# A gate summed on VectorE, spreads by high and low parts, and longer runs of column-tiled products in a two-layer trunk

## The chip, the cores and the metric

The kernel runs on one core of a Trainium2 chip. The core has TensorE (matrix products; PE in the profile, its weight loads PEld), VectorE (DVE), ScalarE (ACT), GpSimd (POOL) and SyncE (SP, which here only issues DMA). The metric is the device time of one execution in microseconds: lower is better. Times of several runs are given as a median with the lowest and highest.

## The reference, cut to what matters

Two layers run over x, 256 tokens of width 1024, all in fp32. In each layer a conditioning vector gives a shift, a scale and a gate, each of 1024 values:

```python
cond = jax.nn.silu(c)
for i in range(DEPTH):                      # DEPTH = 2
    shift, scale, gate = jnp.split(cond @ ada_w[i] + ada_b[i], 3, axis=-1)
    h = rms_norm(x, norm_g[i]) * (1 + scale[:, None, :]) + shift[:, None, :]
    y = nsa_mixer(h, ...) if i % 2 == 0 else moba_mixer(h, ...)
    x = x + gate[:, None, :] * y
```

The first layer's mixer projects h to queries, three kinds of keys and values, branch gates and z. It attends to compressed blocks, to selected blocks and to a window (with 256 tokens the selected blocks and the window both come to causal attention), adds the three with the branch gates, multiplies by silu(z) and projects out. The second layer's mixer has one kind of keys and values and, at this length, is plain causal attention with 16 query heads over 4 key heads of 64, again with silu(z) and an output projection. `cond @ ada_w[i]` reads 12 MB of weights in each layer.

## The kernel before, in words

**Layout.** 128 partitions carry tokens (two tiles `m` of 128) or, where h is transposed (`HT`), channels. Weights come as pieces of 512 KB into a ring of six buffers `raw` (in the opening into twelve buffers `early`). A product of precision fp32 is made of three products of the type fp32r: a value is split into a high part (`hi`, a cast on ScalarE) and a low part (`lo`, a subtraction on VectorE), and high by high, high by low and low by high are added (`parts_of`, `product`). Where a product isn't split, its operands are fp32 and TensorE takes it in that type.

**The conditioning products.** `condz` holds silu(c) as 8 blocks of 128 x 32, of which only the first column isn't zero. `ada_rows` multiplies it with the weights on column tiles: the array is used as four tiles of 128 x 32, so that four products run side by side, each writing 32 rows of PSUM. In the second layer, `ada_ss(1, 0, 4)` and `ada_ss(1, 4, 4)` do scale and shift for one half of the channels each: 8 loads of 2 x 128 rows by 512 columns, 16 products in four groups of four (two of the four tiles hold the even and two the odd steps of the contraction), a copy to SBUF, four transposes, a sum of even and odd, and the affine coefficients `AB`. The first gate, `ada_gate(0)`, goes through `ada_rows` as well; its two rows, each with a bias row under it, are then spread over 128 partitions by two products with `ones` on two row tiles. The second gate, `ada_gate(1)`, is made without TensorE until its end: VectorE multiplies each of 8 pieces of 128 x 1024 by a column of `condz` and adds it into `gate` (GpSimd fills it with zeros first, one row gets the bias), and two fp32 products with `ones` sum over partitions and spread in one.

**Attention.** Heads go in pairs. For each pair: scores, a masked maximum on VectorE, exponentials with their sums on ScalarE, a scaling on VectorE, transposes of the probabilities (`p_transposed`: a copy to `pT`, of which there are five buffers), products with the values on two column tiles of 64 (`values`), and `gated`, which multiplies by z and splits into the parts that the output products read. `pair_a` is the first layer's, `pair_b` the second's.

**Side work.** Generators in the list `side` are advanced one step at a time by `beside()` from the projections and after each pair: before, the order is the compression's products, the first gate, and the two halves of scale and shift; in the second layer, the second gate.

**What sets the order.** Nothing is issued when it is recorded. Every call on `T`, `A`, `V`, `G` and `S` is recorded in `Plan`, with its dependences and a cost by formula (`_cost`), and `issue` then plays the program through on a model of the five engines: at each step it takes the engine whose next operation can begin first, and among the ready operations of one engine the one that begins first, then by rank (level), then by its number. `SHIFT` (the table `LATER_BY`) moves an operation's number in that comparison, `HOLD` keeps it from being taken before a time of the model. Each engine's program is the order that comes out; on the chip, each engine follows it in order and waits on semaphores. SyncE's order is the order of the loads. All these instructions are issued from one line (404), so groups in the profile are told apart by the names of their tiles. A few instructions, such as GpSimd's `memset` of `ones`, aren't recorded but issued at once, and the planner doesn't know when they end. For TensorE the model adds a cost whenever the tiling of the array changes.

Of the kernel before, what the change touches and what calls it, by code (L numbers as in the profile page):

```python
# [37 lines left out]
TILED, LATER, PAUSE = -0.5, 0, 93.0  # L38
# [19 lines left out]
    29: 2400, 32: 3700, 33: 3700, 51: 7200, 312: 35600, 391: 48800, 1276: 152700, 1340: 169100, 1350: 168000,  # L58
    1415: 182100, 1573: 197400, 1576: 198800, 1579: 197400, 1585: 198700, 1636: 205200, 1655: 209300,
# [13 lines left out]
class Plan:  # L73
# [120 lines left out]
    def _cost(self, engine, method, args, kw, aps):  # L194
# [15 lines left out]
        if engine == "T":  # L210
            if method == "transpose":
                return 262.0 if aps[1].dtype == F32 else 180.0
            cols = free(aps[2])
            if aps[2].dtype == F32:
                m, rows = free(aps[1]), aps[1].shape[0]
                if "tile_position" in kw and m * rows <= 64 * P:
                    return max(cols * 4.28 * max(32, m) / P * max(32, rows) / P, 60.0) + (100.0 if rows < P else 0.0)
                return 2 * max(cols * 2.14, 264.0)
            return max(cols * (1.07 if aps[2].dtype == F32R else 1.0), 264.0)
# [31 lines left out]
    def issue(self, opening=()):  # L251
# [51 lines left out]
        while done < len(ops):  # L303
# [58 lines left out]
            if e == "T":  # L362
                tick = int(start // TICK)
                if op["mode"] != mode:
                    cost += 240.0
# [66 lines left out]
def kernel(  # L432
# [129 lines left out]
    nc.gpsimd.memset(ones, 1.0)  # L562
    identR = const.tile([P, P], F32R, name="identR")
# [156 lines left out]

    gates_of = {}

    def ada_gate(l):
# [3 lines left out]
        if l:  # L727
            G.memset(gate, 0.0)
            Q.dma_start(gate[0:1], bias)
            for kk in range(8):  # L730
                w = ada_piece(l, kk, 2 * D, D)[:, 0, :]
                with plan.at(FILL):
                    V.scalar_tensor_tensor(gate, w, condz[:, kk, 0:1], gate, op0=OP.mult, op1=OP.add)
                yield
            mix, src = (ones, ones), (gate[:, 0:512], gate[:, 512:1024])
        else:
            g = yield from ada_rows(l, (2 * D, 2 * D + 512), 512)
            for s in range(2):
                Q.dma_start(g[64 * s + 1:64 * s + 2], bias[:, s * 512:(s + 1) * 512])
            ts = [tile_of("ps", 512) for s in range(2)]  # L740
            with plan.at(FILL):
                with plan.group():
                    for s in range(2):
                        T.matmul(ts[s], ones[64 * s:64 * s + 64], g[64 * s:64 * s + 64], start=True, stop=True,
                                 tile_position=(64 * s, 0))
                for s in range(2):
                    A.copy(gate[:, s * 512:(s + 1) * 512], ts[s])
            return
        for s in range(2):
            t = tile_of("ps", 512)  # L750
            with plan.at(FILL):
                T.matmul(t, mix[s], src[s], start=True, stop=True)
                A.copy(gate[:, s * 512:(s + 1) * 512], t)
# [180 lines left out]
    def values(o, parts, first):  # L934

        with plan.group():
# [271 lines left out]
    side += [cmp_steps(hid), ada_gate(0), ada_ss(1, 0, 4), ada_ss(1, 4, 4)]  # L1208
# [270 lines left out]
    def pair_b(i):  # L1479
# [15 lines left out]
        pT = p_transposed(lambda e, j: pm[0][:, e] if j == 0 else pm[1][:, e, (j - 1) * P:j * P])  # L1495
        o = tile_of("ps", 512)
        vs = slice(g * HD, (g + 1) * HD)
        values(o, [([VB[:, m, vs] for m in range(2)], pT)], True)
        gated(i, o, zT[i])

    for i in range(8):
        pair_b(i)
        beside()
    assert not side
# [36 lines left out]
```

## Time and profile before

| | |
|---|---|
| time, median of 3 runs | 313.22 us (312.3 to 313.4) |
| profiled execution: its own time | 312.48 us |
| profiled execution: span from first to last instruction | 310.7 us |
| TensorE busy | 301.6 us, 97% |
| VectorE busy | 242.0 us, 78% |
| ScalarE busy | 205.1 us, 66% |
| GpSimd busy | 28.2 us, 9% |
| read from memory | 64.36 MB, 211 GB/s over the span |
| granted TensorE clock | 1.00 |

The profile is of one execution. A group's row gives the engine, the operation, the tile that is written, the tiles that are read, the shape, the count, the busy time in us and the mean in ns, and after that the idle time before the group and what ended it. A row of the timeline gives the start, the duration (of merged instructions together), and what they are. A row of stretches gives the stretch, its length, and for PE, PEld, DVE, ACT and POOL the busy time with the number of instructions, then the granted clock, the share of time that the DMA engines were busy, and GB/s. TensorE's instructions overlap, so their durations add up to more than the time that they take.

### The profile page before, as it was taken

The numbers are of one execution on the slowest core, as the hardware profiler recorded it, in microseconds if no ns is written. First come the engines' busy times: TensorE is split into PE (matmuls) and PEld (weight loads), VectorE is DVE, ScalarE is ACT, GpSimd is POOL, SyncE is SP. The second block draws the span as 40 slices with busy tenths as digits, with TensorE's granted clock in tenths as the row PEclk, the third lists the DMA queues.
The fourth block names the chain that finished last, engine by engine and source line by source line (L and its number), as shares of the span: only waits on it lengthen the run. The fifth ranks groups of instructions, "written<-read, shape, count | busy, mean of one in ns | idle before, by whom it ended". The sixth has DMA issues, their size and how long they took to land.

```text
span 310.7 us, 6167 instructions
## 1 busy us (share of the span) xinstructions
PE 301.6 (97%) x2133; PEld 242.0 (78%) x2133; DVE 242.0 (78%) x734; ACT 205.1 (66%) x486; POOL 28.2 (9%) x99
## 2 busy tenths in 40 slices
PE   4999999999999999999999999999999999999995
PEld 4765677768767687976798887787788999987784
DVE  4763483658997399963999989796799999999465
ACT  4735254784845566964999993795585599988520
POOL 8038950000000000000000000000000000000000
PEclk9999999999999999999999999999999999999999
DMA  8999999749999890948925429236288760740002
GB/s 249 321 356 368 366 356 319 223 139 307 331 294 333 282 345 6 329 145 290 309 80 186 153 72 307 96 77 198 69 289 273 225 231 9 263 136 2 0 35 103
DMA packets 44174, 65.82 MB, mean 212 GB/s; under 512 B 4221, under 2 KB 20971, under 8 KB 44142
## 3 DMA queue, kind: packets, MB, share of 16 engines
q1 hardware_dynamic: 43782, 65.36, 64.3%
q8 instruction: 17, 0.28, 0.4%
q14 instruction: 15, 0.12, 0.1%
q10 hardware_dynamic: 168, 0.06, 0.1%
q0 software_dynamic: 192, 0.00, 0.0%
HBM read 64.36 MB, written 1.05 MB: 211 GB/s over the span
## 4 chain that ended last, share of the span: by engine, by line
PE 90%; DVE 3%; DMA 3%; ACT 2%; issue 1%; ACTq 0%; SPq 0%; DVEq 0%
PE ps L404 52%; PE acc L404 38%; DMA y<-in_ada_b_dram 2%; DMA early<-in_nsa_w_in_dram 1%; ACT hi L404 1%; DVE lo L404 1%; DVE rs L404 1%; DVE y L404 0%; ACT n_parts L404 0%; ACTq L404 0%; DVE X L404 0%; DVE p L404 0%; ACT n_out L404 0%; ACT HT L404 0%; DVE n_parts L404 0%
## 5 line engine op out<-in xcount | busy, mean ns | idle before, releaser
L404 ACT CAST hi<-raw 128x1024 fp32r<-128x1024 f32 (+1 forms) x48 | 48.6, 1021 | 24.3 <-PE acc L404 16.5
L404 DVE TENSOR_TENSOR lo<-raw,hi 128x1024 fp32r<-128x1024 f32 (+1 forms) x48 | 56.5, 1182 | 6.5 <-ACT hi L404 6.3
L404 PE MATMUL acc<-hi,HT 128*128 128x512 f32 (+1 forms) x160 | 49.6, 382 | 0.1
L404 ACT ACTIVATE p<-p,tiny 128x128 f32<-128x128 f32 (+1 forms) x96 | 42.9, 451 | 6.5 <-DVE tiny L404 6.2
L404 PE MATMUL acc<-HT,hi 128*128 128x256 f32 x192 | 37.4, 285 | 0.0
L404 DVE CUSTOM_DVE_ANT_0 p<-ps,causal 128x128 f32<-128x128 f32 (+1 forms) x96 | 30.6, 346 | 8.2 <-ACT hi L404 5.6
L404 PEld LDWEIGHTS acc<-hi,HT 128*128 128x128 f32 x160 | 29.1, 188 | 8.0 <-issue 2.5
L404 PEld LDWEIGHTS acc<-HT,hi 128*128 128x128 f32 x192 | 30.2, 189 | 0.5 <-issue 0.5
L404 PE MATMUL acc<-lo,HT 128*128 128x512 f32 (+1 forms) x80 | 30.3, 383 | 0.2
L404 PE MATMUL ps<-hi,HT 128*128 128x512 f32 (+1 forms) x96 | 28.2, 365 | 0.0
L404 PE MATMUL acc<-HT,lo 128*128 128x256 f32 x96 | 27.2, 284 | 0.0
L404 PE MATMUL ps<-KTA,qg 128*128 128x256 f32 (+2 forms) x192 | 26.9, 281 | 0.0
L404 PEld LDWEIGHTS ps<-KTA,qg 128*128 128x128 f32 x192 | 24.0, 189 | 2.7 <-issue 1.7
L404 ACT COPY pT<-ps 128x384 f32<-128x384 f32 x48 | 21.0, 477 | 4.0 <-PE ps L404 4.0
L404 ACT CAST hi<-early 128x1024 fp32r<-128x1024 f32 (+2 forms) x17 | 14.9, 896 | 13.1 <-DMA early<-in_nsa_w_in_dram 8.9
L404 PE MATMUL ps<-hi,qg 128*128 128x256 f32 (+1 forms) x96 | 23.4, 326 | 0.0
L404 DVE TENSOR_TENSOR lo<-early,hi 128x1024 fp32r<-128x1024 f32 (+2 forms) x17 | 17.6, 1047 | 5.9 <-ACT hi L404 5.9
L404 PE MATMUL acc<-hi,qg 128*128 128x512 f32 x64 | 21.7, 405 | 0.0
L404 PE MATMUL ps<-identF,p 128*128 128x128 f32 x144 | 21.2, 274 | 0.0
L404 PEld LDWEIGHTS ps<-hi,HT 128*128 128x128 f32 x96 | 17.0, 188 | 3.5 <-issue 1.2
L404 PEld LDWEIGHTS ps<-identF,p 128*128 128x128 f32 x144 | 16.8, 141 | 2.7 <-issue 0.7
L404 PE MATMUL ps<-pT,VA 128*64 128x256 f32 (+1 forms) x192 | 18.5, 333 | 0.0
(220 smaller groups left out, 614.4 us busy)
## 6 DMA issues: line engine op xcount, KB each, us to landing
raw<-in_ada_w_dram SPq DMA_DIRECT2D x32, 512.0 KB, 5.2
raw<-in_moba_w_in_dram SPq DMA_DIRECT2D x20, 512.0 KB, 4.4
early<-in_ada_w_dram SPq DMA_DIRECT2D x12, 512.0 KB, 9.5
raw<-in_nsa_w_in_dram SPq DMA_DIRECT2D x12, 512.0 KB, 6.8
early<-in_nsa_w_in_dram SPq DMA_DIRECT2D x9, 512.0 KB, 8.8
p<-in_nsa_cmp_w_dram SPq DMA_DIRECT2D x16, 256.0 KB, 4.1
raw<-in_nsa_w_out_dram SPq DMA_DIRECT2D x8, 512.0 KB, 4.8
raw<-in_moba_w_out_dram SPq DMA_DIRECT2D x8, 512.0 KB, 5.2
```

What stands on the lines that cost most here:

```text
L404: r = getattr(self.engines[e], method)(*[self._real(a) for a in args], **{k: self._real(a) for k, a in kw.items()})
```

## The change

- `ada_gate` has one way for both layers: GpSimd fills `gate` with zeros, SyncE loads the bias into its first row, and VectorE adds the 8 pieces. Then `gate` is split into high and low parts, and for each half two products of type fp32r with `onesR`, an fp32r copy of `ones`, sum and spread it (before: two fp32 products in all). `onesR` is made by VectorE at the start.
- `ada_all` takes the place of the two halves `ada_ss(1, ...)`: in each of 8 steps two pieces of 128 x 1024 are loaded, and four products on the four column tiles make the two halves of shift and the two of scale. One copy and four transposes follow, and `AB` is computed from PSUM directly.
- The side work's order in the first layer is now: compression, `ada_all`, `ada_gate(0)`.
- `pair_b` ends with the transposed probabilities; `values_b` makes the products with the values for two pairs in one group, then `gated` for both. `beside()` is still called after each pair.
- The planner's cost of a change of tiling goes from 240 to 440, the costs of tiled fp32 products are other numbers, and the tables `LATER_BY` and `HOLD` are new (the operations' numbers have changed as well).

```diff
-TILED, LATER, PAUSE = -0.5, 0, 93.0
+TILED, LATER, PAUSE, SWITCH = -0.5, 0, 93.0, 440.0
 LATER_BY = [
...
 HOLD = {
-    29: 2400, 32: 3700, 33: 3700, 51: 7200, 312: 35600, 391: 48800, 1276: 152700, 1340: 169100, 1350: 168000,
...
+    88: 15400, 157: 27100, 169: 21500, 248: 16700, 355: 51500, 374: 52700, 390: 46600, 391: 51800, 1044: 118900,
...
 }
@@
                 if "tile_position" in kw and m * rows <= 64 * P:
-                    return max(cols * 4.28 * max(32, m) / P * max(32, rows) / P, 60.0) + (100.0 if rows < P else 0.0)
+                    if rows < P:
+                        return max(cols * 2.02 * max(32, m) / P, 269.0)
+                    return max(cols * 4.03 * max(32, m) / P, 60.0)
@@
                 if op["mode"] != mode:
-                    cost += 240.0
+                    cost += SWITCH
@@
     ones = const.tile([P, P], F32, name="ones")
     nc.gpsimd.memset(ones, 1.0)
+    onesR = const.tile([P, P], F32R, name="onesR")
+    V.tensor_copy(onesR, ones)
     identR = const.tile([P, P], F32R, name="identR")
     V.tensor_copy(identR, identF)
@@
+    def ada_all():
+
+        acc = tile_of("ps", 512)
+        for kk in range(8):
+            w = [ada_piece(1, kk, c0, D)[:, 0] for c0 in (0, D)]
+            with plan.at(FILL), plan.group():
+                for s in range(2):
+                    for h in range(2):
+                        j = 2 * s + h
+                        T.matmul(acc[32 * j:32 * j + 32], condz[:, kk], w[s][:, 512 * h:512 * h + 512],
+                                 start=(kk == 0), stop=(kk == 7), tile_position=(0, 32 * j))
+            if kk < 7:
+                yield
+        g = tile_of("row", 512)
+        A.copy(g, acc)
+        t = tile_of("ps", 512)
+        with plan.group():
+            for q in range(4):
+                T.transpose(t[:, q * P:(q + 1) * P], g[:, q * P:(q + 1) * P], identF)
...
+        V.tensor_add(a_, tv[:, 1], rt(ROW_ADA + 32))
+        V.scalar_tensor_tensor(a_, a_, 1.0, rt(ROW_G + 8), op0=OP.add, op1=OP.mult)
+        V.tensor_add(b_, tv[:, 0], rt(ROW_ADA + 24))
@@
-        if l:
-            G.memset(gate, 0.0)
-            Q.dma_start(gate[0:1], bias)
-            for kk in range(8):
...
-            mix, src = (ones, ones), (gate[:, 0:512], gate[:, 512:1024])
-        else:
-            g = yield from ada_rows(l, (2 * D, 2 * D + 512), 512)
-            for s in range(2):
-                Q.dma_start(g[64 * s + 1:64 * s + 2], bias[:, s * 512:(s + 1) * 512])
...
-                        T.matmul(ts[s], ones[64 * s:64 * s + 64], g[64 * s:64 * s + 64], start=True, stop=True,
-                                 tile_position=(64 * s, 0))
...
+        G.memset(gate, 0.0)
+        Q.dma_start(gate[0:1], bias)
+        for kk in range(8):
+            w = ada_piece(l, kk, 2 * D, D)[:, 0, :]
             with plan.at(FILL):
-                T.matmul(t, mix[s], src[s], start=True, stop=True)
+                V.scalar_tensor_tensor(gate, w, condz[:, kk, 0:1], gate, op0=OP.mult, op1=OP.add)
+            yield
+        hi, lo = parts_of(gate.rearrange("p (s n) -> p s n", s=2))
+        for s in range(2):
+            t = tile_of("ps", 512)
+            with plan.at(FILL):
+                with plan.group():
+                    T.matmul(t, onesR, hi[:, s], start=True, stop=False)
+                    T.matmul(t, onesR, lo[:, s], start=False, stop=True)
                 A.copy(gate[:, s * 512:(s + 1) * 512], t)
@@
-        with plan.group():
+        with nullcontext() if plan.open else plan.group():
@@
-    side += [cmp_steps(hid), ada_gate(0), ada_ss(1, 0, 4), ada_ss(1, 4, 4)]
+    side += [cmp_steps(hid), ada_all(), ada_gate(0)]
@@
-        pT = p_transposed(lambda e, j: pm[0][:, e] if j == 0 else pm[1][:, e, (j - 1) * P:j * P])
-        o = tile_of("ps", 512)
-        vs = slice(g * HD, (g + 1) * HD)
-        values(o, [([VB[:, m, vs] for m in range(2)], pT)], True)
-        gated(i, o, zT[i])
-
-    for i in range(8):
-        pair_b(i)
+        return i, p_transposed(lambda e, j: pm[0][:, e] if j == 0 else pm[1][:, e, (j - 1) * P:j * P])
+
+    def values_b(pairs):
+
+        os = [tile_of("ps", 512) for _ in pairs]
+        with plan.group():
+            for o, (i, pT) in zip(os, pairs):
+                values(o, [([VB[:, m, i // 2 * HD:(i // 2 + 1) * HD] for m in range(2)], pT)], True)
+        for o, (i, _) in zip(os, pairs):
+            gated(i, o, zT[i])
+
+    for i in range(0, 8, 2):
+        pairs = [pair_b(i)]
         beside()
+        pairs.append(pair_b(i + 1))
+        beside()
+        values_b(pairs)
```

More of the change, by code (lines that the diff above doesn't have):

```diff
@@ L1 @@
-from contextlib import ExitStack, contextmanager
+from contextlib import ExitStack, contextmanager, nullcontext
 import concourse.bass as bass
@@ L57 @@
 HOLD = {
-    29: 2400, 32: 3700, 33: 3700, 51: 7200, 312: 35600, 391: 48800, 1276: 152700, 1340: 169100, 1350: 168000,
-    1415: 182100, 1573: 197400, 1576: 198800, 1579: 197400, 1585: 198700, 1636: 205200, 1655: 209300,
[3 rows of a table added]
 }
@@ L719, in ada_ss, with rt @@
         V.tensor_add(b_, tv[:, :, 0], RT[:, b:b + nk])
+    def ada_all():
[16 more added lines that the diff above has]
+                T.transpose(t[:, q * P:(q + 1) * P], g[:, q * P:(q + 1) * P], identF)
+        tv = t.rearrange("p (q s h z) -> p s h q z", q=4, s=2, h=2)[:, :, :, :, 0]
+        a_, b_ = (AB[1][:, s].rearrange("p (h q) -> p h q", h=2) for s in range(2))
+        def rt(at):
+            return RT[:, at:at + 8].rearrange("p (h q) -> p h q", h=2)
+        V.tensor_add(a_, tv[:, 1], rt(ROW_ADA + 32))
+        V.scalar_tensor_tensor(a_, a_, 1.0, rt(ROW_G + 8), op0=OP.add, op1=OP.mult)
+        V.tensor_add(b_, tv[:, 0], rt(ROW_ADA + 24))
     gates_of = {}
@@ L726, in ada_gate @@
         bias = bass.AP(tensor=ada_b.tensor, offset=ada_b.offset + l * 3 * D + 2 * D, ap=[[D, 1], [1, D]])
-        if l:
-            G.memset(gate, 0.0)
-            Q.dma_start(gate[0:1], bias)
-            for kk in range(8):
[L731 to L734, printed above, removed]
-            mix, src = (ones, ones), (gate[:, 0:512], gate[:, 512:1024])
-        else:
-            g = yield from ada_rows(l, (2 * D, 2 * D + 512), 512)
-            for s in range(2):
-                Q.dma_start(g[64 * s + 1:64 * s + 2], bias[:, s * 512:(s + 1) * 512])
-            ts = [tile_of("ps", 512) for s in range(2)]
-            with plan.at(FILL):
-                with plan.group():
-                    for s in range(2):
-                        T.matmul(ts[s], ones[64 * s:64 * s + 64], g[64 * s:64 * s + 64], start=True, stop=True,
-                                 tile_position=(64 * s, 0))
-                for s in range(2):
-                    A.copy(gate[:, s * 512:(s + 1) * 512], ts[s])
-            return
+        G.memset(gate, 0.0)
+        Q.dma_start(gate[0:1], bias)
+        for kk in range(8):
+            w = ada_piece(l, kk, 2 * D, D)[:, 0, :]
+            with plan.at(FILL):
+                V.scalar_tensor_tensor(gate, w, condz[:, kk, 0:1], gate, op0=OP.mult, op1=OP.add)
+            yield
+        hi, lo = parts_of(gate.rearrange("p (s n) -> p s n", s=2))
         for s in range(2):
@@ L934, in values @@
     def values(o, parts, first):
-        with plan.group():
+        with nullcontext() if plan.open else plan.group():
             for n, (v, pT) in enumerate(parts):
```

31 rows, old and new, of tables (HOLD, LATER_BY) are left out of this document.

## The prediction, made before the result was known

> **What bounds the kernel now.** I read the head of the page first (busy times, then the chain that ended last), then the busy times by stretch, then TensorE's instructions in order of time.
>
> ```profile
> span 310.7 us, 6167 instructions
> PE 301.6 (97%) x2133; PEld 242.0 (78%) x2133; DVE 242.0 (78%) x734; ACT 205.1 (66%) x486; POOL 28.2 (9%) x99
> PE 90%; DVE 3%; DMA 3%; ACT 2%; issue 1%; ACTq 0%; SPq 0%; DVEq 0%
> ```
>
> TensorE is busy 97% of the span and is 90% of the chain that ended last. "Busy" could hide waiting, so I looked at distances between starts: twelve plain products of 512 columns, all of the same kind,
>
> ```profile
> 202.38 2.97 PE L404 MATMUL acc<-KTA,HT 128*128 128x512 f32 x12
> 205.19 1.55 PE L404 MATMUL acc<-n_parts,HT 128*128 128x512 f32 x6
> ```
>
> take 2.81 us to the next start, 0.234 us each, and are given as busy 0.16 us beyond it. So distances between starts, not durations, are the price of work on TensorE, and I use them throughout. Then by stretch: duration, then PE, PEld, DVE and ACT busy.
>
> ```profile
> 0.00:60.00 60.00, 55.60 (x381) 40.59 (x382) 34.42 (x88) 29.22 (x48) 28.20 (x99) 1.00 1.00 322
> 60.00:192.00 132.00, 131.49 (x1011) 103.17 (x1010) 107.90 (x373) 97.88 (x259) 0.00 (x0) 1.00 0.69 228
> 110.00:130.00 20.00, 20.00 (x179) 17.40 (x178) 19.15 (x93) 14.70 (x47) 0.00 (x0) 1.00 0.57 201
> 130.00:150.00 20.00, 20.00 (x179) 14.47 (x178) 11.14 (x53) 12.80 (x41) 0.00 (x0) 1.00 0.74 256
> 150.00:180.00 30.00, 30.00 (x241) 26.03 (x241) 30.00 (x121) 29.09 (x91) 0.00 (x0) 1.00 0.50 158
> 180.00:192.00 12.00, 12.00 (x87) 9.63 (x86) 10.36 (x19) 8.90 (x18) 0.00 (x0) 1.00 0.59 178
> ```
>
> From 60 us on TensorE hardly stops. Two readings matter: work taken off TensorE shortens the run about one for one, as long as nothing else takes the lead; and the engine that would take it is VectorE, full from 150 to 180 us while TensorE is full too.
>
> **The change part by part.**
>
> *First gate off TensorE.* Each step of the conditioning products is a group of four products on 32 columns each, recorded as eight instructions:
>
> ```profile
> 68.27 1.07 PE L404 MATMUL ps<-raw,condz 128*32 128x512 f32 x8
> 69.26 0.41 PE L404 MATMUL acc<-hi,HT 128*128 128x304 f32 x1
> ...
> 103.36 1.92 PE L404 MATMUL ps<-raw,condz 128*32 128x512 f32 x16
> 105.22 1.21 PE L404 MATMUL ps<-KTA,qg 128*128 128x256 f32 x8
> ...
> 108.97 1.13 PE L404 MATMUL ps<-row,ones 64*128 64x512 f32 x4
> 110.03 0.44 PE L404 MATMUL ps<-identF,g 128*128 128x128 f32 x2
> ```
>
> A group alone takes 0.99 us until the next start (68.27 to 69.26), two together 1.86. The side work runs in its written order, so of the twelve groups the first four are the first gate's: three runs of one, and half of the run at 103.36. That is 3 x 0.99 + 0.93 = 3.90 us. The two products that spread the gate take 1.06 us more (108.97 to 110.03). In their place come four products of 512 columns with `onesR`, at 0.234 us: 0.94 us. Net **-4.0 us**.
>
> *Second gate.* Its two full-precision spreads stand in the second layer's attention, among the values' runs that I need as well:
>
> ```profile
> 261.29 0.87 PE L404 MATMUL ps<-pT,VA 128*64 128x256 f32 x8
> 262.09 0.50 PE L404 MATMUL acc<-HT,hi 128*128 128x256 f32 x2
> ...
> 270.65 2.37 PE L404 MATMUL ps<-pT,VA 128*64 128x256 f32 x24
> 272.95 2.13 PE L404 MATMUL ps<-KTA,qg 128*128 128x256 f32 x16
> ...
> 281.90 1.10 PE L404 MATMUL ps<-gate,ones 128*128 128x512 f32 x2
> 282.93 1.52 PE L404 MATMUL ps<-pT,VA 128*64 128x256 f32 x16
> 284.38 0.66 PE L404 MATMUL ps<-KTA,qg 128*128 128x128 f32 x4
> ...
> 285.96 1.02 PE L404 MATMUL ps<-gate,ones 128*128 128x512 f32 x2
> 286.82 0.49 PE L404 MATMUL ps<-identF,p 128*128 128x128 f32 x3
> ...
> 288.83 1.56 PE L404 MATMUL ps<-pT,VA 128*64 128x256 f32 x16
> ```
>
> 1.03 + 0.86 = 1.89 us become 0.94: **-0.95 us**. The split into high and low parts adds one ScalarE cast and one VectorE subtraction at a place from which nothing waits until the second layer's output products come back.
>
> *Values in longer runs.* Eight instructions are one pair of heads. The planner already joins pairs: the runs are of one, three, two and two pairs, four in all, and the change writes four runs of two. A run of one takes 0.80 us, one of two 1.45, so joining saves 0.80 + 0.80 - 1.45 = 0.15 us a time. Between all eight apart and all joined that is at most 0.6 us either way; with four runs before and after I take **0**. The next pairs' transposed probabilities have one spare buffer of five until a double run ends; the first consumer needs both pairs of a group anyway, so nothing later is pushed back by more than the second half of a run, 0.65 us, behind which the output products stand as cover.
>
> *Scale and shift in one go.* 16 loads and eight groups of four products, as before, only each group now takes one row block with its four column tiles. Four of eight transposes leave, and an evacuation on ScalarE:
>
> ```profile
> 128.92 0.62 PE L404 MATMUL ps<-identF,row 128*128 128x128 f32 x4
> 129.38 1.15 PE L404 MATMUL ps<-identF,p 128*128 128x128 f32 x9
> ```
>
> **-0.46 us**. The loads have rows twice as long; between 60 and 192 us the DMA share is 0.69, so I count nothing for that. TensorE's total: 4.0 + 0.95 + 0.46 = 5.4 us less.
>
> *What VectorE gets.*
>
> ```profile
> L404 DVE SCALAR_TENSOR_TENSOR gate<-raw,condz,gate 128x1024 f32<-128x1024 f32 x8 | 10.2, 1279 | 2.2 <-DMA raw<-in_ada_w_dram 2.2
> L404 DVE TENSOR_TENSOR lo<-raw,hi 128x1024 fp32r<-128x1024 f32 x44 | 53.3, 1218 | 4.3 <-ACT hi L404 4.1
> L404 DVE TENSOR_TENSOR y<-acc,gate x4: 683/691/692, 192.8 to 302.8; 128x512 f32<-128x512 f32 x4
> ```
>
> The second gate's accumulation shows the first's price: 8 x 1.279 = 10.2 us, and 1.22 for the low part, 11.4 us, all before the first layer's gate is first used, at 192.8 us. A few small instructions of the second half of scale and shift leave; not counted. Its fill on GpSimd (0.95 us, a row below) and its one bias load run early, with those engines free; two small bias loads into `row` leave. The eight loads move behind the sixteen of scale and shift in SyncE's queue; each now holds a raw buffer until VectorE has multiplied it, and later weight loads stand behind that in the queue. Does it fit? From 60 to 192 us VectorE would be busy 107.9 + 11.4 = 119.3 us of 132 - 4.5 = 127.5: it fits. But the gate's pieces are last in line, so perhaps little of it comes before 110 us: from there VectorE has 19.15 + 11.14 + 30.00 + 10.36 = 70.65 us, with the gate 82.0, while TensorE has 82 - 4.5 = 77.5. The bounds of what is given back are therefore 0 and 4.5 us. From 150 to 180 us both engines are full without TensorE stopping, so a full VectorE alone does not stall it, and from 130 to 150 us VectorE has 8.9 us free. I take **+1.2 us**, nearer to zero.
>
> *`onesR`.* The copy is recorded ahead of `identR` with the same level and no shift in the table, so it becomes VectorE's first instruction; and it reads `ones`, which GpSimd fills late.
>
> ```profile
> 1.40 0.61 DVE L404 CAST identR<-identF 128x128 fp32r<-128x128 f32 x1 [1.40 <-POOL identF masks.py:199]
> 3.21 0.17 DVE L404 COPY RT<-ps 128x8 f32<-128x8 f32 x1 [1.20 <-PE ps L404]
> 4.15 0.20 POOL L562 MEMSET ones<- 128x128 f32 x1
> 4.27 0.21 ACT L404 ACTIVATE sg<-RT 128x8 f32<-128x8 f32 x1
> 4.29 0.95 POOL L404 MEMSET gate<- 128x1024 f32 x1
> 4.51 0.76 DVE L404 TENSOR_SCALAR sg<-sg 128x8 f32<-128x8 f32 x1 [1.13 <-ACT sg L404]
> 12.57 0.50 PE L404 MATMUL acc<-hi,HT 128*128 128x512 f32 x1
> ```
>
> Queued behind it are `identR`, `emask` and the copy of `c` (RT), for which ScalarE's `sg` waits, and behind `sg` the squares of x, the row scales, and so the first products at 12.57 us. The first copy can start at 4.35 and, with 0.61 us as for `identR` and as much again for the two behind it, RT moves from 3.21 to about 5.6 and `sg` from 4.27 to about 5.7: up to 1.4 us late. Where the first products wait for the weights anyway, nothing. Between 0 and 1.4 I take **+0.7 us**.
>
> The row of `sg` on VectorE shows more: an instruction of eight elements takes 0.76 us and ends at 5.27, just as GpSimd's fill of `gate` ends (5.24). The Trainium skill (SBUF — State Buffer, Who interferes with whom) says that a VectorE copy or scalar operation using both ports and a GpSimd instruction shut each other out for a whole instruction; this trace agrees. By that page `onesR` could have to wait until 5.24, and the sum would be up to 0.9 us longer; the sum above leaves this out.
>
> *The reordered opening.* The planner's table, holds and switch cost are new, so the first loads come in another order. TensorE has 4.4 us free in the first 60 us, which bounds a gain; a loss I bound by the same amount, since the loads' amount is unchanged. I take **0**, and one microsecond either way for the range.
>
> **Sum.** -5.4 + 1.2 + 0.7 = -3.5 us from the profiled execution's own 312.48 us (1.8 us around the span): **309.0 us**. The median of the runs is 313.22, 0.7 us above that execution, so against the median the same saving is 309.7; I keep 309.0.
>
> **The rivals.**
>
> *Nothing is given back.* VectorE's free 8.9 us from 130 to 150 take the gate, `onesR` is hidden by waiting for weights: 312.5 - 5.4 = **307.1 us**. For it: TensorE's share of the chain. Against: this needs VectorE near 94% over the stretch.
>
> *VectorE becomes the bound in the first attention.* The whole 4.5 us comes back and the start-up's 1.4 is only partly hidden (0.7): 312.5 - 5.4 + 4.5 + 0.7 = **312.3 us**, no change. For it: the full 150 to 180 us. Against: VectorE waits there for nothing that TensorE hasn't given, and its subtractions of later weights can move.
>
> *Slower: weight loads stand behind the gate's buffers.* Six raw buffers, eight gate pieces, and each is freed only when a low-priority VectorE instruction has run; SyncE issues in order, so a z or output weight behind them is issued late.
>
> ```profile
> raw<-in_nsa_w_out_dram SPq DMA_DIRECT2D x8, 512.0 KB, 4.8
> ```
>
> A weight issued when it is already wanted costs its landing, 4.8 us. Two such: 312.5 - 5.4 + 0.7 + 9.6 = **317.4 us**; it decides once more than one landing is exposed. Against: the DMA share is 0.50 from 150 to 180 us, so loads have room to go early.
>
> That the values' runs don't get longer in fact is part of the forecast: it is worth nothing there.
>
> **How the numbers follow.** Forecast 0.55 (its own range 307.5 to 311.5), nothing given back 0.20, VectorE bound 0.14, late loads 0.11. A measurement of this kernel tells about 0.5% from no change, 1.6 us: faster means under 311.7. Faster: 0.51 of the forecast, 0.20, and 0.05 of the VectorE case: 0.76. Within: 0.04 + 0.09 + 0.02 = 0.15. Slower: 0.09. The range runs from 305.8 (nothing given back, the opening a little better) to 313.0 (VectorE bound, the opening a little worse); late loads and worse are left out.
>
> **What would show it.** In the profile after: 64 instead of 96 instructions `ps<-raw,condz`, no `row,ones`, and eight `onesR` products about 0.23 us apart; sixteen `gate<-raw,condz,gate` on VectorE; the first `RT` copy near 5.6 us and the first product near 13.3 to 14; TensorE's distances unbroken from 110 to 192 us, with waits on VectorE of one or two microseconds there. Waits on DMA for `raw` would make the prediction wrong upwards; a first layer that ends 5 us earlier with no waits, downwards.

## The result, and the profile after

The changed kernel takes 310.56 us (median of 14 runs), the kernel before beside it 313.26 (14 runs): a ratio of 0.9911, 95% interval 0.9894 to 0.9929. It is 2.7 us faster, where 3.5 were forecast from the profiled execution of before. The time lies in the forecast's own range (307.5 to 311.5). One of the 14 executions took 578.19 us and counts in no ratio; the median without it is 310.39 us.

The head of the page of its profiled execution (span, busy times, and the chain that ended last by engine):

```profile
span 310.7 us, 6091 instructions
PE 300.9 (97%) x2097; PEld 244.3 (79%) x2097; DVE 250.9 (81%) x740; ACT 205.1 (66%) x486; POOL 30.8 (10%) x100
PE 80%; DVE 10%; DMA 5%; ACT 2%; issue 1%; SPq 1%; ACTq 0%; DVEq 0%
```

VectorE's share of the chain went from 3% to 10%. The span is that of before, though, and TensorE's busy time is hardly lower. This execution took 312.43 us, longer than most of its kernel. The windows (duration; PE, PEld, DVE, ACT and POOL busy; granted clock of TensorE, DMA share, GB/s) say why, and two instructions that can be found again in another execution say how much it cost:

```profile
120.00:122.00 2.00, 2.00 (x21) 2.00 (x19) 2.00 (x12) 1.79 (x6) 0.00 (x0) 1.00 0.66 264
122.00:124.00 2.00, 2.00 (x15) 2.00 (x15) 2.00 (x7) 1.73 (x9) 0.00 (x0) 0.52 0.02 4
124.00:126.00 2.00, 2.00 (x15) 2.00 (x14) 1.97 (x6) 1.18 (x4) 0.00 (x0) 0.63 0.00 0
126.00:128.00 2.00, 2.00 (x21) 2.00 (x20) 0.10 (x1) 1.91 (x5) 0.00 (x0) 1.00 0.49 133
...
111.91 1.92 PE L412 MATMUL ps<-raw,condz 128*32 128x512 f32 x16
131.91 0.60 PE L412 MATMUL ps<-identF,row 128*128 128x128 f32 x4
```

From 122 to past 125 us TensorE ran at half its clock. "Busy" doesn't show that, since a slow product is just a longer one. So the same kernel was profiled again, and the readings below are from that execution, of 310.52 us:

```profile
span 308.8 us, 6092 instructions
PE 299.5 (97%) x2097; PEld 243.1 (79%) x2097; DVE 250.7 (81%) x740; ACT 205.1 (66%) x486; POOL 30.7 (10%) x100
PE 76%; DVE 14%; DMA 3%; issue 2%; ACT 2%; SPq 1%; ACTq 0%; DVEq 0%
```

Here the clock is full from 13 us to the end. Its windows over the stretches shown of before, and rows of its TensorE in order of time:

```profile
60.00:192.00 132.00, 131.18 (x984) 104.48 (x983) 117.04 (x378) 98.18 (x259) 0.00 (x0) 1.00 0.69 228
110.00:130.00 20.00, 20.00 (x174) 16.41 (x174) 18.55 (x82) 13.62 (x41) 0.00 (x0) 1.00 0.52 169
130.00:150.00 20.00, 20.00 (x173) 16.96 (x174) 20.00 (x69) 15.72 (x47) 0.00 (x0) 1.00 0.72 254
150.00:180.00 30.00, 29.80 (x231) 25.08 (x229) 29.70 (x108) 25.89 (x86) 0.00 (x0) 1.00 0.45 141
```

```profile
67.59 1.08 PE L412 MATMUL ps<-p,p 128*64 128x256 f32 x8
111.56 1.92 PE L412 MATMUL ps<-raw,condz 128*32 128x512 f32 x16
130.06 0.60 PE L412 MATMUL ps<-identF,row 128*128 128x128 f32 x4
171.66 0.39 PE L412 MATMUL ps<-hi,onesR 128*128 128x512 f32 x1
171.88 0.39 PE L412 MATMUL ps<-lo,onesR 128*128 128x512 f32 x1
201.00 0.74 PE L412 MATMUL acc<-KTA,HT 128*128 128x512 f32 x2
```

Two readings. The time at half clock cost (131.91 - 111.91) - (130.06 - 111.56) = 1.50 us between the same two instructions. And VectorE, which had 8.9 us free from 130 to 150 us, is now full there: the first gate's eight pieces are multiplied between 130.3 and about 160 us.

I cut the span at the first `p,p` product (67.25 before, the first row below; 67.59 now) and at the first output product `KTA,HT` (202.38 before, 201.00 now):

| | before | now | difference |
|---|---|---|---|
| start to `p,p` | 67.25 | 67.59 | +0.34 |
| `p,p` to `KTA,HT` (first layer's attention) | 135.13 | 133.41 | -1.72 |
| `KTA,HT` to the end of the span | 108.3 | 107.8 | -0.5 |

```profile
67.25 1.08 PE L404 MATMUL ps<-p,p 128*64 128x256 f32 x8
```

The question is the middle row. Summed from start to next start, the products that the change touches take 4.25 us less there: `raw,condz` 11.41 to 7.69, `row,ones` 1.06 to 0, the transposes of `row` 0.95 to 0.44, the new `onesR` products 1.03. Yet the stretch is only 1.72 us shorter. Where are the other 2.5?

Where the relief falls matters for this. The products of `raw` and `condz` before and now (count; shortest, median and longest in ns; first and last start in us):

```profile
L404 PE MATMUL ps<-raw,condz x96: 592/593/618, 68.3 to 147.9; 128*32 128x512 f32 x96
L412 PE MATMUL ps<-raw,condz x64: 592/592/617, 68.6 to 127.9; 128*32 128x512 f32 x64
```

The first gate's groups are gone, but groups of scale and shift have moved into their places: four single groups start at 68.61, 87.89, 95.16 and 99.42 us, and by 129 us both kernels have done eight groups. What TensorE no longer has is the last four, from 138 to 148 us.

### The profile page after: what moved, and what is told of

The parts are those of the page before. It is cut to its first block, busy times and chain, and to the rows that moved or that the text cites. A ratio compares the mean times of both kernels' runs of the same rounds, so it can differ in the third digit from the quotient of the medians.

```text
span 310.7 us, 6091 instructions
## 1 busy us (share of the span) xinstructions
PE 300.9 (97%) x2097; PEld 244.3 (79%) x2097; DVE 250.9 (81%) x740; ACT 205.1 (66%) x486; POOL 30.8 (10%) x100
## 4 chain that ended last, share of the span: by engine, by line
PE 80%; DVE 10%; DMA 5%; ACT 2%; issue 1%; SPq 1%; ACTq 0%; DVEq 0%
PE ps L412 46%; PE acc L412 35%; DVE p L412 4%; DVE gate L412 2%; DMA y<-in_ada_b_dram 2%; DMA p<-in_nsa_cmp_w_dram 2%; DMA early<-in_ada_w_dram 1%; DVE lo L412 1%; SPq L412 1%; DVE tiny L412 1%; DVE pc L412 1%; DVE qg L412 0%; DVE g L412 0%; ACT n_out L412 0%; ACT HT L412 0%
## 5 line engine op out<-in xcount | busy, mean ns | idle before, releaser
L412 ACT CAST hi<-raw 128x1024 fp32r<-128x1024 f32 (+1 forms) x48 | 48.9, 1024 | 14.9 <-PE acc L412 12.0
L412 PE MATMUL acc<-HT,hi 128*128 128x256 f32 x192 | 40.3, 292 | 0.0
L412 PEld LDWEIGHTS acc<-HT,hi 128*128 128x128 f32 x192 | 31.3, 193 | 2.9 <-issue 2.9
L412 DVE CUSTOM_DVE_ANT_0 p<-ps,causal 128x256 f32<-128x256 f32 (+1 forms) x96 | 30.8, 351 | 0.5 <-PE ps L412 0.3
L412 PE MATMUL acc<-HT,lo 128*128 128x256 f32 x96 | 28.2, 295 | 0.0
L412 ACT CAST hi<-early 128x1024 fp32r<-128x1024 f32 (+2 forms) x17 | 14.8, 891 | 17.2 <-DMA early<-in_nsa_w_in_dram 14.2
L412 PE MATMUL ps<-identF,p 128*128 128x128 f32 x144 | 22.3, 281 | 0.1
L412 DVE SCALAR_TENSOR_TENSOR gate<-raw,condz,gate 128x1024 f32<-128x1024 f32 x16 | 20.3, 1270 | 0.0
L412 PEld LDWEIGHTS acc<-HT,lo 128*128 128x128 f32 x96 | 18.5, 193 | 0.5 <-issue 0.4
```

Of the source, the lines that this page charges most:

```text
L412: r = getattr(self.engines[e], method)(*[self._real(a) for a in args], **{k: self._real(a) for k, a in kw.items()})
```

## The experiments

Times are compared through the ratio to the kernel before on the same chip; such a ratio is known to a quarter of a per cent or worse. Where both kernels have the same order of instructions, the starts of the same instruction in the two traces are compared as well; that shows the place.

**The changed kernel again.** No edit.

> The changed kernel once more, for a profile without the dip of the granted clock (0.83 from 120 to 130 us in the first one). Theory (VectorE gives back about 2 us between 131 and 161 us, the start-up costs 0.4 to 1.0, and the dip is chance): 2.7 us faster than before (309.8 to 311.0), TensorE at its full clock throughout, and the chain of waits from 131 to 161 us still mostly VectorE. Rival (the new order itself brings the clock down there): the dip from 120 to 130 us is there again.

310.06 us, ratio 0.9899 (0.9874 to 0.9924), no dip of the clock in the profile. So the order doesn't bring the dip with it every time. The chain of waits from 128 to 165 us is 31% VectorE's `p`, 18% its `gate`, and only 20% TensorE.

**The first gate's sum made thin.**

```diff
-                V.scalar_tensor_tensor(gate, w, condz[:, kk, 0:1], gate, ...)
+                V.scalar_tensor_tensor(gate[:, 0:8], w[:, 0:8], condz[:, kk, 0:1], gate[:, 0:8], ...)   # first gate only
```

> The changed kernel with the first gate's eight accumulations on VectorE over 8 of 1024 columns; its loads, waits and order stay (it leaves out most of the first gate's sum). VectorE is relieved of 8 x about 1.2 us = 9 to 9.6 us. Theory (VectorE is the bound from 131 to 161 us and gives back 1.7 to 2.5 us): 1.7 to 2.5 us faster than the changed kernel. The prediction's own term: 1.2 us faster. Rival (VectorE's work is hidden): within 0.3 us. Rival (VectorE bounds the whole of the first attention): 4 us or more faster.

Ratio 0.9872 (0.9842 to 0.9903), which the interval doesn't separate from 0.9899. The trace does: TensorE's rows at the two cuts, and the window in which VectorE was full:

```profile
66.48 1.08 PE L412 MATMUL ps<-p,p 128*64 128x256 f32 x8
198.49 0.73 PE L412 MATMUL acc<-KTA,HT 128*128 128x512 f32 x2
...
131.00:161.00 30.00, 30.00 (x272) 26.66 (x272) 25.34 (x113) 23.17 (x75) 0.00 (x0) 1.00 0.68 227
```

The stretch takes 132.01 us instead of 133.41. Instruction by instruction the lead is constant to 140 us, grows by 1.4 us until 175, and is constant again. So VectorE's accumulations cost 1.4 us. But with these gone, 4.25 us less of TensorE's work still gives only 3.12 (135.13 - 132.01): another 1.1 us went elsewhere. That is known to within some 0.7 us: the stretch took 135.86 us in another execution of the old order with the same TensorE work, and 133.55 and 133.87 us in two more of the new order (the runs of the start-up below).

**TensorE relieved in the kernel before.** Does its work count one for one at all? Nine of the twelve side groups were made thin there, with nothing added to VectorE.

```diff
-                            T.matmul(acc[32 * j:32 * j + 32, :n], condz[:, k, :], w[s][:, k % step, :], ...)
+                            T.matmul(acc[32 * j:32 * j + 32, :64], condz[:, k, :], w[s][:, k % step, :64], ...)   # kk > 1
```

> The kernel before with nine of its twelve side groups of conditioning products (72 of the 96 products of raw and condz) over 64 instead of 512 columns; order, loads and waits stay (it leaves out most of the first gate and of the second layer's scale and shift). The 96 products took 11.40 us of TensorE's time between their starts, 0.119 each; at 64 columns 72 of them should take about 0.03 each, so TensorE is relieved of about 6.4 us and VectorE gets nothing more to do. Theory (TensorE alone sets the pace before, relief counts one for one): 6 to 6.8 us faster than before. Rival (some of the relief is lost to waits whoever does the work, so that the missing part of the change's gain is not VectorE's and the new order's): 4.5 us faster or less.

311.12 us, ratio 0.9931 (0.9911 to 0.9951): 2.1 us, where the theory said 6 to 6.8. TensorE's rows at the cuts, ScalarE's waits from 74 to 106 us in this kernel and then in the kernel before (total, times, longest), and the windows of before and of this kernel:

```profile
67.13 1.08 PE L404 MATMUL ps<-p,p 128*64 128x256 f32 x8
201.46 2.97 PE L404 MATMUL acc<-KTA,HT 128*128 128x512 f32 x12
...
ACT hi L404 <- DMA raw<-in_nsa_w_in_dram: 6.0, 2, 3.7
```

```profile
ACT hi L404 <- PE acc L404: 6.1, 3, 3.9
...
67.00:110.00 43.00, 43.00 (x295) 30.33 (x293) 33.45 (x82) 26.66 (x51) 0.00 (x0) 1.00 0.90 302
```

```profile
120.00:126.00 6.00, 5.83 (x67) 5.15 (x65) 6.00 (x28) 3.76 (x10) 0.00 (x0) 1.00 0.41 122
126.00:130.00 4.00, 3.20 (x22) 3.13 (x22) 3.54 (x11) 3.48 (x11) 0.00 (x0) 0.59 1.02 367
```

The products take 6.5 us less (11.41 to 4.93 from start to start), the stretch 0.8 us less. Not all of the difference has to do with the relief. From 77 to 81 us, ahead of the first thin group at 88.59 us, this execution falls 1.0 us behind the one of before, at casts and compression products that wait for weights. From there the first three thin groups win 2.1 us, 1.1 us of it is lost by 103 us at compression products whose weights aren't there, and at 112 us the two are level. The run with only the copy of the ones (below) has the order of before, no relief and a later TensorE, and it loses 0.7 us near 96 us to the same weights:

```profile
96.13 0.19 PEld L404 LDWEIGHTS ps<-p,p 128*64 128x64 f32 x2 [0.85 <-DMA p<-in_nsa_cmp_w_dram]
```

So on DMA engines 90% busy weights come earlier in one execution and later in another. That an earlier TensorE only meets them earlier is argued here, not shown. The next three thin groups win another 2.2 us by 125 us. Then TensorE waits 0.8 us for VectorE's `n_parts`, its clock falls (0.59 from 126 to 130 us), and at 130 us it is 0.5 us behind before. The mean granted clock was 0.988 to 0.994 in all six timed executions. What the timed runs show is enough against my theory of one for one: 6.5 us of relief give 2.1 us, 1.5 to 2.8 by the interval.

**Only the last three groups thin.** The same edit for the groups between 139 and 148 us.

> The kernel before with only the last three of the nine thinned groups thinned (those from 139 to 148 us, of the second layer's scale and shift, which is left out in part); the six from 87 to 125 us are whole again. TensorE is relieved of about 2.2 us in place of 6.5. Theory (the six earlier groups were worth nothing: the weights of the input projection and of the compression hold TensorE until 104 us, and at 122 us a wait for VectorE lets the granted clock fall, which costs what was won): granted clock back at 0.998 or more in all runs, and 1.0 to 2.2 us faster than before, so about as fast as with nine groups thinned. Rival (relief counts wherever it is, and the clock in the run with nine groups was chance): a third of 2.1, so 0.7 us faster, with clocks of 0.994 as there.

311.88 us, ratio 0.9962 (0.9939 to 0.9985), 1.2 us faster; mean clock 0.997 to 1.0 in ten of twelve executions.

```profile
67.12 1.08 PE L404 MATMUL ps<-p,p 128*64 128x256 f32 x8
200.82 2.98 PE L404 MATMUL acc<-KTA,HT 128*128 128x512 f32 x12
...
PE ps L404 <- ACT pT L404: 0.5, 1, 0.5
```

A third of the relief (2.2 us) shortens the stretch by 1.4 us (133.70), more in this trace than nine thin groups did; in the timed runs it gives 1.2 of the 2.1. The six earlier groups, 4.3 us of TensorE, were thus worth about 0.9 us by the timed runs, uncertain by as much again. And even the late relief isn't whole: at 148 us the lead was 2.4 us, and at 152 it is 1.5, lost to one wait for transposed probabilities (the last row above, from 144 to 160 us) and to small gaps, where VectorE was full already before the change (150 to 180 us).

**The start-up, three ways.** The copy of the ones alone, put into the kernel before:

```diff
-    nc.gpsimd.memset(ones, 1.0)
+    nc.gpsimd.memset(ones, 1.0); onesR = ...; nc.vector.tensor_copy(onesR, ones)
```

> The kernel before with only the copy of the ones to float32r added as VectorE's first instruction (its result is not used). Theory: the first product moves from 12.57 to about 14.0 us, and the kernel is 0.35 to 0.5 us slower than before, what is not absorbed by 67 us. Rival 1 (the start-up counts in full): 1.3 to 1.5 us slower. Rival 2 (absorbed): within 0.2 us of before.

314.36 us, ratio 1.0042 (1.0021 to 1.0063): 1.3 us slower, between 0.7 and 2.0, so the first rival. Then the wait taken out of the changed kernel, first by filling `ones` as GpSimd's first act, then by copying it only before the first gate's first accumulation:

```diff
-    ones = ...; nc.gpsimd.memset(ones, 1.0)          # after the masks
+    ones = ...; nc.gpsimd.memset(ones, 1.0)          # ahead of identF
```

> The changed kernel with GpSimd filling the tile of ones before it makes the identity, so that VectorE's first instruction, the copy of the ones to float32r, does not wait 4.4 us. Nothing else moves. Theory (the stall pushes the first product by 1.46 us, of which 0.35 is left at 67 us): the first product is back at about 12.6 us and the kernel 0.35 to 0.5 us faster than the changed one. Rival 1 (the whole 1.46 us counts): 1.3 to 1.5 us faster. Rival 2 (the opening is bound by its loads): no difference (within 0.2 us).

```diff
-    V.tensor_copy(onesR, ones)                        # VectorE's first instruction
+    nc.vector.tensor_copy(onesR, ones)                # before the first gate's accumulation for kk = 0
```

> The changed kernel with the copy of the ones to float32r taken from the head of VectorE's order and put right before the first gate's first accumulation (about 130 us); nothing else moves. So VectorE waits for nothing at the start and has 0.9 us less to do there. Theory (the stall costs what it cost the kernel before, 1.3 us): 0.8 to 1.5 us faster than the changed kernel, ratio to before 0.985 to 0.987, the first product of the input projection at about 12.6 us. Rival (the changed kernel's opening takes most of it up, as with the ones filled first): within 0.4 us of the changed kernel, ratio 0.989 to 0.990.

Ratios 0.9887 (0.9859 to 0.9914) and 0.9916 (0.9882 to 0.9949): neither differs from the changed kernel's 0.9899. The traces show a little more. The first `p,p` product came at 66.46 to 66.93 us in the three profiled executions of the new order without the wait, on average 66.75, and at 66.48 to 67.88 in six with it (this kernel twice and the edits that leave the opening alone), on average 67.37: 0.6 us, in a scatter of 1.4. In the old order it came at 67.12 to 67.25 without the copy (three) and here with it:

```profile
68.44 0.87 PE L404 MATMUL ps<-p,p 128*64 128x256 f32 x6
```

1.3 us later. One difference between the orders is ScalarE's wait for weights from 14 to 67 us: in the kernel before, in before with the copy, in the changed kernel, in the one with the late copy, and in the one with the thin gate, which has the copy in its first place:

```profile
ACT hi L404 <- DMA early<-in_nsa_w_in_dram: 8.0, 2, 5.8
```

```profile
ACT hi L404 <- DMA early<-in_nsa_w_in_dram: 8.4, 2, 5.7
```

```profile
ACT hi L412 <- DMA early<-in_nsa_w_in_dram: 15.0, 4, 5.1
```

```profile
ACT hi L412 <- DMA early<-in_nsa_w_in_dram: 20.2, 4, 6.1
```

```profile
ACT hi L412 <- DMA early<-in_nsa_w_in_dram: 19.0, 4, 6.1
```

In the new opening the casts wait for weights much longer. Whether 15 or 20 us doesn't go with the copy, though. Of the six executions with the copy in its place, three wait 14.2 to 15.0 us and have their first product of the input projection at 14.03 to 14.44 us; the other three wait 19.0 to 20.7 and have it at 12.75 to 13.14. What tells these apart is TensorE's own speed from 9.5 to 12.7 us, first the changed kernel, then the one with the thin gate:

```profile
9.55 1.08 PE L412 MATMUL ps<-identF,n_in 128*128 128x128 f32 x4 [0.68 <-DVE rs L412]
9.56 0.63 PE L412 MATMUL ps<-identF,n_in 128*128 128x128 f32 x4 [1.25 <-DVE rs L412]
```

The same four transposes take 1.08 and 0.63 us: in the first three executions TensorE comes to its full clock only near 13 us, in the other three by 9 us. (The windows give the clock as 1.00 there; the trace's record of it begins only with the full clock.) No run shows whether the copy has a part in that. Among executions with the early clock, the first product is at 12.89 us on average with the copy and at 12.19 (12.02 to 12.35) in the three without the wait: 0.7 us, of which a part is lost again to waits for weights. That the reordered opening hides half of the stall or more is thus argued: 0.6 us in the new order against 1.3 in the old, the first within its scatter.

**The spreads in full precision again.**

```diff
-                    T.matmul(t, onesR, hi[:, s], start=True, stop=False)
-                    T.matmul(t, onesR, lo[:, s], start=False, stop=True)
+                    T.matmul(t, ones, gate[:, s * 512:(s + 1) * 512], start=True, stop=True)   # hi, lo not made
```

> The changed kernel with both gates spread by one fp32 product of the ones for each half, as the second gate was before, in place of two float32r products of its high and low parts; the parts are not made. TensorE has 2 x about 0.95 us more, VectorE 2 x 1.22 and ScalarE 2 x 1.05 us less. Theory (TensorE sets the pace at both spreads): 1.2 to 1.9 us slower than the changed kernel, the steps at the products of ones near 172 and 288 us. Rival (the parts' making on VectorE and ScalarE costs as much as the shorter products save): within 0.4 us.

311.62 us, ratio 0.9938 (0.9919 to 0.9957) against 0.9899: 1.2 us slower. By the starts, the first gate's spread costs 0.5 us (VectorE and ScalarE win a little back there) and the second's 0.7.

**The values pair by pair again.**

```diff
-        with plan.group():
-            for o, (i, pT) in zip(os, pairs):
-                values(...)
+        for o, (i, pT) in zip(os, pairs):
+            values(...)                    # each pair its own group
```

> The changed kernel with the second layer's values recorded pair by pair again, not two pairs in one group; the planner is free to put them next to each other. Prediction's own term (it already ran them in four runs before, so the longer runs give nothing): within 0.4 us of the changed kernel, and four runs of values in the trace. Rival (each group more costs a change of TensorE's tiling): 0.5 to 1.2 us slower than the changed kernel.

311.62 us, ratio 0.9944 (0.9926 to 0.9962): 1.4 us slower, and not four runs but eight, the first and the last of them here:

```profile
262.53 0.87 PE L413 MATMUL ps<-pT,VA 128*64 128x256 f32 x8
...
286.67 0.87 PE L413 MATMUL ps<-pT,VA 128*64 128x256 f32 x8
```

With the new table the planner doesn't join the pairs by itself, and four runs more cost 1.6 us by the starts, some 0.4 each. A run's price isn't in its own products alone. Two runs of one take 0.15 us more than one of two (0.80 + 0.80 against 1.45), as forecast; but the plain product ahead of a run and the one behind it are also longer to the next start, 0.21 or 0.22 us instead of 0.12 for 256 columns and 0.33 instead of 0.23 for 512, so 0.1 us on either side. The order around the runs changed too in this run, so the 1.6 isn't theirs alone for certain. Against the kernel before, which had four runs, the change wins nothing by it, but without the group it would have lost. The rival was right on the price of a run, the prediction on the change.

**The first gate's sum on GpSimd.** A version that might beat both: GpSimd is idle there.

```diff
-                V.scalar_tensor_tensor(gate, w, condz[:, kk, 0:1], gate, ...)
+                nc.gpsimd.tensor_scalar_mul(w, w, condz[:, kk, 0:1])                # first gate only
+                nc.gpsimd.tensor_add(gate, gate, w)
```

> The changed kernel with the first gate's eight accumulations on GpSimd, each as a product in place and a sum, in place of VectorE's eight; every other engine keeps its order. VectorE is relieved of 8 x about 1.28 us, as in the run with the thin gate, whose products came 1.36 us earlier by 175 us. Theory (VectorE's work from 131 to 161 us is what holds TensorE, and GpSimd is idle there): 1.0 to 1.5 us faster than the changed kernel. Rival (GpSimd's operations keep VectorE waiting, as the opening suggests, or the gate comes too late): no faster, or slower by up to 5 us, with VectorE's own operations longer while GpSimd works.

327.56 us, ratio 1.0446 (1.0423 to 1.0470), 17 us slower than the changed kernel, all between 133 and 170 us. VectorE's groups from 130 to 176 us in this kernel, then in the changed one (busy and mean ns behind the bar):

```profile
L412 DVE TENSOR_SCALAR p<-p,tiny 128x256 f32<-128x256 f32 x13 | 16.2, 1282 | 0.0
L412 DVE CUSTOM_DVE_ANT_0 p<-ps,causal 128x256 f32<-128x256 f32 x14 | 5.6, 417 | 1.4 <-PE ps L412 1.2
L412 DVE TENSOR_TENSOR lo<-raw,hi 128x1024 fp32r<-128x1024 f32 x2 | 5.0, 2482 | 0.0
```

```profile
L412 DVE CUSTOM_DVE_ANT_0 p<-ps,causal 128x256 f32<-128x256 f32 x21 | 8.1, 420 | 0.0
L412 DVE TENSOR_TENSOR lo<-raw,hi 128x1024 fp32r<-128x1024 f32 x5 | 6.1, 1229 | 0.0
L412 DVE TENSOR_SCALAR p<-p,tiny 128x256 f32<-128x256 f32 x18 | 5.8, 356 | 0.0
```

While GpSimd works, VectorE's scalings of `p` take 1282 ns instead of 356 and the subtractions 2482 instead of 1229; those that read the accumulators stay at 417. TensorE waits 9 us for VectorE's results there. The clock has a share too: it is 0.50 from 142 to 148 us and 0.64 from 148 to 154, some 10 us at half, so up to 5 of the 17 us (an estimate from these two windows). An idle GpSimd isn't free for VectorE.

**Scalings on ScalarE.** The other engine with room, busy 22 of 30 us from 131 to 161 us.

```diff
-                V.tensor_scalar_mul(p[:, e, 0], p[:, e, 0], sm[:, 1, e, r:r + 1])
+                nc.scalar.activation(p[:, e, 0], p[:, e, 0], AF.Copy, scale=sm[:, 1, e, r:r + 1])   # pairs 1 to 6, r = 0
```

> As the run with the late copy of the ones, and twelve of the 32 scalings of the first attention's p by a column (pairs 1 to 6, one of the two tiles of the second half of the rows) put from VectorE to ScalarE at the same place in the order. VectorE is relieved of 12 x about 0.28 = 3.4 us between 131 and 180 us; ScalarE, busy 22 of 30 us there, gets 12 x about 0.45 = 5.4 us. Theory (VectorE holds TensorE from 131 to 161 us): 0.5 to 1.2 us faster than the run with the late copy, the products of the first attention that much earlier by 175 us. Rival (ScalarE's queue is in order, and the scalings hold up the exponentials and copies behind them): no faster, or slower by up to 3 us, with ScalarE as the releaser of TensorE's waits.

310.26 us, ratio 0.9907 (0.9880 to 0.9934): the same as the late copy alone. Against that run, by the starts, it gains 0.5 us from 130 to 160 us and loses 0.3 by 167 and 0.7 at 177, where a product waits for a copy in ScalarE's queue (waits from 172 to 182 us):

```profile
PEld ps L412 <- ACT pT L412: 0.9, 1, 0.9
```

The rival's mechanism, at the size that cancels the gain. No version was found that is measurably faster than the changed kernel.

## Why the prediction was right, and which of its sizes were wrong

Direction, range and likeliest case held; 309.0 was 1.6 us too low. Part of that is the base: the sum was made from an execution of 312.48, and before's medians are 313.26 and 312.80. Against the median the prediction itself gave 309.7; the rest is 0.9 us. The full range had an easy task: 305.8 to 313.0 also holds the second rival's 312.3, which is no change.

- **First gate and scale and shift, -4.46 of TensorE's time.** As work this was right: 4.25 by the starts. The step that failed is the reading ahead of it: "work taken off TensorE shortens the run about one for one". In the old order 6.5 us of relief won 2.1, and the last 2.2 of them 1.2 in the timed runs and 1.4 in the trace. The prediction priced the first gate's groups where they stood (68, 88, 94 and 103 us) and didn't ask where the relief would fall. In the new order others stand there, and the groups that are gone are those from 138 to 148 us, the place of the late thin groups, next to a VectorE that is full from 150 us on. Of the change's own 4.25 us, 3.12 arrived without VectorE's new work, a share like that of the late thin groups. That the missing 1.1 is of the same kind, small gaps behind a full VectorE, is argued from that run in the old order; no run isolates it in the new one, and none separates what the new tables give or cost by themselves.
- **VectorE's give-back, +1.2.** Right: 1.4 by the thin gate, between 140 and 175 us. It was put at 1 to 2 us from 110 to 192, and the bound of 4.5 stayed far off.
- **`onesR`, +0.7.** Right as to what waits for what: the first `RT` copy came at 5.51 to 5.53 in all six executions, forecast 5.6. The first product at 14.03 and 14.10, forecast 13.3 to 14, is partly luck, since TensorE was slow there until 13 us; the other three have it at 12.75 to 13.14. One step of the path was missed. VectorE's `sg`, which took 0.76 us beside GpSimd's fill and ended at 5.27 before, now comes behind the fill and takes 0.17:

```profile
5.95 0.17 DVE L412 TENSOR_SCALAR sg<-sg 128x8 f32<-128x8 f32 x1 [0.28 <-ACT sg L412]
```

  So what follows `sg` is 0.85 us late and not 1.4. The 0.6 us by the traces fits the term, though the timed runs can't tell it from nothing. The same stall costs 1.3 in the old opening; if the new one does hide a part, "the reordered opening, 0" and this term aren't independent.
- **Second gate, -0.95.** About -0.5 between the two profiles, 0.7 when undone.
- **Values in longer runs, 0.** Right as a difference; four runs before and after. But its bound of 0.6 between all apart and all joined was too small: it priced the runs' own products and not the 0.1 us in the product on either side, and eight runs cost 1.4 us more than four in the timed runs, 1.6 by the starts.
- **The rivals.** VectorE as the bound was right for 30 us, not for the whole stretch, and so for 1.4 us instead of 4.5. Nothing given back fell with the two losses. Late weights behind the gate's buffers didn't appear: no such wait stands among TensorE's.

So -4.25 + 1.4 + 1.1 in the middle stretch, +0.34 ahead of it and -0.5 behind it give the -1.9 us by which the two spans differ (310.7 and 308.8); the medians differ by 2.7, and single executions of the changed kernel vary from 309.1 to 311.2 at full clock.

## What to carry to other kernels

Before pricing work taken off the busiest engine, ask of each place what would be late next there, and read the transfers' share and the other engines' load in that stretch, not over the whole: here a thinning of 6.5 us of TensorE's work won 2, and the last third of it 1.2. When work goes and the rest moves up, the relief falls where the last of it stood, not where the removed part stood. Price a change of tiling with the products on both sides of it. A stall priced in one order of work may cost something else in another; price it where it will stand. An engine that looks idle may still be paid for by its neighbours.

## What the runs showed of the hardware

- **TensorE's clock fell without a pause of its length.** In the first profile after, the clock is half for 3.4 us from 122.0 us. No two products in the 7 us ahead of it start more than 0.26 us apart, but from 120.29 on there are sixteen of only 32 columns, 0.11 us apart, so TensorE may have had little to multiply:

```profile
120.29 1.85 PE L412 MATMUL ps<-KTA,qg 128*128 128x32 f32 x16
```

  In the run with nine thin groups sixteen such products and a gap of 1.06 us come before it, and the dip is about as long. The Trainium skill (TensorE: Matmul & The Clock Gate, What's actually happening) gives half the clock after an idle window of about 3.4 us, with windows that run freely. The length agrees; by this trace the cause isn't idleness alone. That small products count as little activity is argued from these two places and wasn't tried. Freely running windows would fit that one execution of the same order has the dip and another not.
- **VectorE waits for GpSimd by kind of operand.** In the run with the sum on GpSimd, single scalings of `p` (SBUF to SBUF) took from 0.34 to 2.51 us, 3.6 times their usual time on average, and the two subtractions of 1024 columns twice theirs; the longest scalings end within 0.2 us of the end of a GpSimd addition that was running. What reads the accumulators wasn't longer (the groups above). The Trainium skill (SBUF — State Buffer, Who interferes with whom) says so of two-port operations and, beside a GpSimd instruction that reads SBUF, of those with two SBUF inputs, and this run agrees for these groups. It doesn't for the subtractions `qg<-g,qg` of 256 columns, which have two SBUF inputs: four took 412 ns on average against 424 in the changed kernel, three of them beside a GpSimd instruction. At the start the wait shows as well: `onesR` took 0.93 us and ended within 0.1 us of GpSimd's fill, where 0.23 us was enough with `ones` filled first.
